# A sixth seven-product pair in the second wide gate of a hybrid encoder layer, with the turning of one block of m moved into that gate

## The chip, the cores and the metric

The kernel runs on one core of one Trainium2 chip. The metric is the time of one execution on the device in microseconds (us). Three executions of the kernel before the change took 1293.12, 1293.61 and 1294.81 us, a median of 1293.61 us. One further execution was recorded by the hardware profiler; all rows of the trace come from that one.

## The reference

One layer on 256 tokens of width 2048, then a final RMSNorm. Only the part around the change is needed:

```python
h = rms_norm(x, g_norm)
proj = h @ w_in                     # uv | q,k,v | gates (2 x 2048 columns)
y_a = gmlp_branch(uv, ...)          # 1024 wide
y_b = neighbourhood_attn(q, k, v, rpb)   # 1024 wide
g_a, g_b = split(sigmoid(gates), 2)
merged = g_a * (y_a @ w_branch[:1024]) + g_b * (y_b @ w_branch[1024:])
x = x + merged @ w_out
x = x + conv_ffn(rms_norm(x))       # up-projection, width-3 convolution, SiLU gate, down-projection
```

Everything is float32. `m` below is `merged`, and a "wide gate" is the right half (1024 of 2048 columns) of `h @ w_in` for `g_a` or `g_b`, before its sigmoid.

## The kernel before, in words

**Products.** A float32 product is made of three TensorE matmuls on halves of the operands (`triple`, L317 to L319: high·high, low·high, high·low). A raw piece of weights `wraw` comes by DMA; ScalarE copies its high part to `whi` (L170), VectorE subtracts to get `wlo` (L171). Activations stand in the same two parts (`h0` to `h7`, a pair of 128-row blocks of k each).

**Steps.** All weights are cut into pieces, numbered through the whole kernel. `begin(i)` issues the load of piece i+5, writes the split of a piece some steps ahead (4 in the wide gates), and then the tasks that were put down for step i by `at(i, ...)`. No scheduler reorders anything: each engine executes its instructions in the order in which the code writes them, step by step. So the number in an `at` decides behind which splits, sums and matmuls a task stands on VectorE, ScalarE, TensorE and in the DMA queue of SyncE (SP).

**A wide gate** (`wide`, `run_wide`) computes 256 x 1024 outputs over k = 2048: 16 pieces of 128 x 1024, taken as 8 pairs in the order of `GATE_ORDER`. C[t][c] are four accumulator banks (row block t, column half c). A plain piece writes four triples, C00, C01, C10, C11, so a plain pair has 24 matmuls. A pair in `GATE_QUADS` (numbered by place) takes seven block products instead of eight, 21 matmuls: in its first piece P0, C00 and C01, in its second P1, P3, P2 and C10, into four more banks P; C11 gets nothing from such a pair. The PSUM pool has 8 banks. When the last such pair is done, `post_sums` (L590 to L594, one ScalarE copy and four VectorE operations) takes P into the gate's tile; `add_sums` (L599, four VectorE operations) adds C at the end of the gate, and a sigmoid (L925) follows on ScalarE.

**Sums for a seven-product pair.** The operands are sums of blocks. Those of the activations are made earlier and kept in DRAM; `kept_sums` reads them back (L1225, tile `s`, 512 KB on SP's queue). Those of the weights are made at the pair by four VectorE additions of 128x512 (`weight_sums`: L363, L364 into `t13`, L360, L361 into `t24`) three pieces ahead, and split two pieces ahead (`weight_sums_split`: ScalarE L374 into h13, h24; VectorE L375 into l13, l24). For the k-pairs 0 and 3 the split weight sums come ready from DRAM instead (`split_read`, L1217, tiles `kh13` and so on), at leads given by `GATE_SPLIT`.

**m.** `ev_branch` multiplies a branch product with its gate, one 512-column block j at a time; for br = 1 it adds the two (`g`, here `g1`). `turn_m(j)` then turns the block: for each half `k2`, four 128x128 transposes on TensorE (L958) into one bank, a ScalarE copy `f` for the later sums (L963), two ScalarE copies of the high parts of `m` (L526) and two VectorE subtractions of the low parts (L531). For block j = 1 this stood at the step ahead of the first piece of the second wide gate: `g_gw[1][1]` is the number of that piece.

Around the change the program goes: first wide gate (gate 0), second wide gate (gate 1), then the remaining branch products, and much later `merged @ w_out`, which reads `m`.

Of the kernel before, what the change touches and what calls it, by code (L numbers as in the profile page):

```python
# [49 lines left out]
GELU_AT = (21, 18)  # L50
X_SUMS = ((1, 5, 6), (2, 12, 13), (6, 18, 19))
GATE_KEPT, GATE_MADE = (1, 2, 6), (0, 3, 4)
GATE_QUADS = ((0, 1, 2, 4, 5, 6), (1, 2, 4, 5, 6))
GATE_ORDER = ((2, 3, 0, 1, 4, 5, 10, 11, 12, 13, 6, 7, 8, 9, 14, 15), (10, 11, 2, 3, 0, 1, 14, 15, 4, 5, 6, 7, 12, 13, 8, 9))
GATE_SPLIT = ({0: (2, 4, 3), 3: (2, 3, 2)}, {0: (2, 4, 3), 3: (2, 1, 1)})
GATE_FIRST = (40, (44, 46, 48, 48), (49, 51))
GATE_JOB = (3, (6, 6, 7, 7), (9, 12))
GATE_SUMS = ((0, 38, 40, "y4", "y5"), (3, 39, 40, "y6", "y7"))
GATE_LATE, Y_LATE = 7, 44
KEEP_AT = (22, 25, 29)  # L60
OUT_PAIRS = (0, 1, 2, 3, 4)
# [17 lines left out]
def trunk_kernel(ctx, tc, x, x_t, vecs, w_in, ln_g, ln_b, w_st, b_s, rpb, w_branch, w_out, w_up, w_down,  # L79
# [26 lines left out]
    def bank():  # L106
        return psum.tile([128, 512], F32, name="bank")
# [10 lines left out]
    def plan_wide(src, row0, order, c0):  # L118
        first = len(pieces)
        for k in order:  # L120
            pieces.append((src, row0 + k * 128, 2, (c0, 512, 1, 0), 512))
        return first
# [66 lines left out]
    def at(i, f):  # L189
        tasks.setdefault(i, []).append(f)  # L190
# [90 lines left out]

    def wide(src, row0, order, c0, acts, quads, room, done, sums=None, stored=None, split=None, late=False, lead=4):
        n0 = plan_wide(src, row0, order, c0)
        boxes = {}
        for q in quads:
            i = n0 + 2 * q
            k = order[2 * q]
            units[i], units[i + 1] = 1, 2  # L290
            b = boxes[q] = {}
            ready = split[0].get(k // 2) if split else None
            if stored:
                b["acts"] = {}
                at(i - (ready[0] if ready else lead), lambda b=b, k=k: stored(k // 2, b["acts"]))
            else:
                b["acts"] = sums[k]
            if ready:
                halved.add(i)
                for n, lead in zip(("13", "24"), ready[-2:]):  # L300
                    at(i - lead, lambda b=b, k=k, n=n: split[1](k // 2, b, n))
                continue
            whole[i] = whole[i + 1] = None
            halves = late and q == quads[0]
            at(i - 3, lambda i=i, b=b, halves=halves: weight_sums(i, b, room, halves))
            if halves:
                at(i - 2, lambda b=b: b.pop("rest")())
            at(i - 2, lambda b=b: weight_sums_split(b, room))
        return ("wide", n0, order, acts, quads, boxes, done)

    def sum_acts_at(i, j, box, pair, room, name, early=False):
# [42 lines left out]
    def weight_sums(i, box, room, halves=False):  # L354
        r0, r1 = whole.pop(i), whole.pop(i + 1)
        t13, t24 = room("t13", F32), room("t24", F32)
        box["w"] = (t13, t24)

        def rest():
            nc.vector.tensor_add(t24[:, 1], t13[:, 0], r1[:, 1])  # L360
            nc.vector.tensor_add(t24[:, 0], r1[:, 0], t24[:, 1])  # L361

        nc.vector.tensor_add(t13[:, 0], r0[:, 0], r0[:, 1])  # L363
        nc.vector.tensor_add(t13[:, 1], r0[:, 1], r1[:, 1])  # L364
        if halves:
            box["rest"] = rest
        else:
            rest()

    def weight_sums_split(box, room):  # L370
        u = []
        for name, t in zip(("13", "24"), box.pop("w")):
            h, l = room("h" + name, F32R), room("l" + name, F32R)
            nc.scalar.activation(h, t, AF.Copy)  # L374
            nc.vector.tensor_sub(l, t, h.bitcast(F32))  # L375
            u.append((h, l))
        split_sums(box, u)

    def split_sums(box, u):
        box["t"] = {1: [x[:, 0] for x in u[0]], 3: [x[:, 1] for x in u[0]],  # L380
                    2: [x[:, 1] for x in u[1]], 4: [x[:, 0] for x in u[1]]}
# [205 lines left out]
    def post_sums(P, x, spare):  # L587
        p1, p5, p6, p7 = P
        (x11, x12), (x21, x22) = x
        nc.scalar.activation(x11, p1, AF.Copy)  # L590
        nc.vector.tensor_sub(spare, x11, p6)
        nc.vector.tensor_add(x12, p5, spare)
        nc.vector.tensor_add(x21, p7, spare)
        nc.vector.tensor_add(x22, p5, x21)  # L594
# [301 lines left out]
    def gate_tile(br):  # L896
        mg["t", br] = mg["p"].tile([128, NT, 1024], F32, name=f"g{br}")
# [10 lines left out]
    def ev_gate_sums(br):  # L908
        def done(P, i):
            def go():  # L910
                gate_tile(br)
                mg["x", br] = [[mg["t", br][:, t, c * 512:(c + 1) * 512] for c in range(2)] for t in range(NT)]
                post_sums(P, mg["x", br], junk)

            at(i + 1, go)
        return done

    def ev_gate_wide(br):
        def done(ps, i):
            g = mg["t", br]  # L920
            add_sums(ps, mg["x", br])

            def sigmoid():
                for t in range(NT):
                    nc.scalar.activation(g[:, t, :], g[:, t, :], AF.Sigmoid, scale=st1["r"][:, t:t + 1])  # L925

            at(i + 1, sigmoid)
            for c in range(2):
                mg[br, 2 + c] = g[:, :, c * 512:(c + 1) * 512]
        return done  # L930

    def ev_branch(br, j):
        def done(ps, i):
            g = mg[br, j]
            for t in range(NT):
                nc.vector.tensor_mul(g[:, t, :], ps[t], g[:, t, :])
            if br == 1:
                for t in range(NT):
                    nc.vector.tensor_add(g[:, t, :], g[:, t, :], mg[0, j][:, t, :])
                at(i + 1 if j == 3 else g_gw[1][1] - 1 if j == 1 else i + 2, lambda: turn_m(j))  # L940
        return done

    def open_m(half):
# [4 lines left out]

    mg["mT"], mg["pairs"] = [], []

    def turn_m(j):
        g = mg[1, j]
        for k2 in range(2):
            p = bank()
            for kk in range(2):
                c = k2 * 2 + kk
                for t in range(NT):
                    nc.tensor.transpose(p[:, kk * T + t * 128:kk * T + (t + 1) * 128],  # L958
                                        g[:, t, c * 128:(c + 1) * 128], ident)
            k = j * 4 + k2 * 2  # L960
            if k // 2 in OUT_PAIRS:
                f = mg["f", k // 2] = mg["fp"].tile([128, 512], F32, name=f"f{k // 2}")
                nc.scalar.activation(f, p, AF.Copy)  # L963
            split_pair(p, mg["mT"][k:k + 2], None)
# [227 lines left out]
    for n, (q, i, j) in enumerate(X_SUMS):  # L1192
        sum_acts_at(i, j, first_sums[2 * q], lambda q=q: q,
                    lambda name, dt, i=i: first_room("s2" if name == "f" and i < 16 else name, dt), f"s{n}", True)
# [27 lines left out]
    def kept_sums(pair, box):  # L1222
# [3 lines left out]
        box["s"] = sums_of(o)  # L1226

    g_gw = [wide(w_in2, 0, GATE_ORDER[br], (GA0, GB0)[br] + 1024, xt, GATE_QUADS[br], sums_room,
                 (ev_gate_sums(br), ev_gate_wide(br)), stored=kept_sums, lead=2,
                 split=(GATE_SPLIT[br], split_read(g_kept, br, lambda pair, name: sums_room("k" + name, F32R), nc.sync)))  # L1230
            for br in range(2)]
    g_m2 = [g_branch(br, j) for j in (2, 3) for br in range(2)]
# [53 lines left out]
    for n, (pair, g) in enumerate((pair, g) for g in range(2) for pair in OUT_SPLIT[g]):  # L1286
        t_kept[pair, g] = split_rows("out", pair, g)
        i = g_at[2 * n][1]
        split_ahead(w_o, t_kept, lambda: at_pool["jobs"], lambda c: f"th{c}", nc.sync, pair, g, g * 1024, i + OUT_JOB[0], [i + a for a in OUT_JOB[1]],
                    [i + a for a in OUT_JOB[2]], 4, last=True)  # L1290
    for n, (pair, br) in enumerate((pair, br) for br in range(2) for pair in GATE_SPLIT[br]):
        g_kept[pair, br] = split_rows("gate", pair, br)
# [66 lines left out]
    def down_order(g):  # L1359
# [194 lines left out]
```

## Time and profile before

| | |
|---|---|
| median of three executions | 1293.61 us (1293.12 to 1294.81) |
| the profiled execution | 1293.75 us, its span 1292.0 us |
| TensorE busy | 1281.9 us of the span |
| VectorE busy | 1140.6 us |
| ScalarE busy | 814.2 us |
| gate 0's last two pieces | 411.93 to 418.26 us |
| gate 1 | 418.26 to 458.38 us |

Times in the trace are in microseconds from the start of the span; a row gives its start, its length, engine, line, operation, output and inputs, and in brackets the idle time before it and what ended it. The executions' times are 1.75 us above the span in the profiled one; that difference lies outside the program's instructions. The profile names lines of the kernel before; in the changed kernel the same statements stand one to five lines lower (L318 to L320 for a triple, L172 for `wlo`, L361 to L365 for the weight sums, L376 for their low parts, L532 for the low parts of `m`, L600 for `add_sums`, L963 for a transpose).

### The profile page before, as it was taken

The numbers are of one execution on the slowest core, as the hardware profiler recorded it, in microseconds if no ns is written. First come the engines' busy times: TensorE is split into PE (matmuls) and PEld (weight loads), VectorE is DVE, ScalarE is ACT, GpSimd is POOL, SyncE is SP. The second block draws the span as 40 slices with busy tenths as digits, with TensorE's granted clock in tenths as the row PEclk, the third lists the DMA queues.
The fourth block names the chain that finished last, engine by engine and source line by source line (L and its number), as shares of the span: only waits on it lengthen the run. The fifth ranks groups of instructions, "written<-read, shape, count | busy, mean of one in ns | idle before, by whom it ended". The sixth has DMA issues, their size and how long they took to land.

```text
span 1292.0 us, 19677 instructions
## 1 busy us (share of the span) xinstructions
PE 1281.9 (99%) x6656; PEld 1093.1 (85%) x6656; DVE 1140.6 (88%) x1707; ACT 814.2 (63%) x1228; POOL 174.6 (14%) x309
## 2 busy tenths in 40 slices
PE   9999999999999999999999999999999999999997
PEld 7888888888888888888888888888888888888885
DVE  7898978888889988997888899898988989989988
ACT  7776577877855645566566656566665656555654
POOL 0003806334000001100001001100000001211210
PEclk9999999999999999999999999999999999999999
DMA  9789879998899977975588788888866859998993
GB/s 368 273 269 280 276 251 301 330 313 299 280 331 355 365 258 239 412 228 163 180 295 274 238 299 292 267 266 286 268 219 221 278 173 360 370 390 320 359 385 142
DMA packets 200182, 370.56 MB, mean 287 GB/s; under 512 B 16017, under 2 KB 124177, under 8 KB 200081
## 3 DMA queue, kind: packets, MB, share of 16 engines
q1 hardware_dynamic: 175616, 287.02, 64.9%
q0 software_dynamic: 23888, 81.23, 17.9%
q8 instruction: 52, 0.85, 0.3%
q10 hardware_dynamic: 576, 1.06, 0.2%
q14 instruction: 50, 0.40, 0.1%
HBM read 321.53 MB, written 45.61 MB: 284 GB/s over the span
## 4 chain that ended last, share of the span: by engine, by line
PE 99%; ACT 0%; DVE 0%; issue 0%
PE bank L222 31%; PE bank L226 16%; PE bank L317 12%; PE bank L319 12%; PE bank L318 12%; PE bank L250 5%; PE bank L252 5%; PE bank L251 5%; PE bank L829 1%; PE bank L879 0%; PE bank L493 0%; PE bank L693 0%; PE bank L869 0%; PE bank L1033 0%; PE bank L958 0%; ACT x L1159 0%
## 5 line engine op out<-in xcount | busy, mean ns | idle before, releaser
L171 DVE TENSOR_TENSOR wlo<-wraw,whi 128x1024 fp32r<-128x1024 f32 (+1 forms) x472 | 538.4, 1153 | 103.6 <-ACT whi L170 69.7
L170 ACT ACTIVATE whi<-wraw 128x1024 fp32r<-128x1024 f32 (+1 forms) x472 | 463.8, 996 | 194.3 <-PE bank L318 88.2
L222 PE MATMUL bank<-h,whi 128*128 128x512 f32 x1760 | 425.5, 392 | 0.0
L222 PEld LDWEIGHTS bank<-h,whi 128*128 128x128 f32 x1760 | 322.0, 188 | 61.8
L226 PEld LDWEIGHTS bank<-h,wlo 128*128 128x128 f32 x1760 | 225.9, 191 | 8.8
L226 PE MATMUL bank<-h,wlo 128*128 128x256 f32 x1760 | 228.6, 283 | 0.0
L1059 ACT ACTIVATE tc<-ta,ck 128x256 f32<-128x256 f32 x86 | 47.1, 595 | 110.4 <-DVE ta L1057 110.4
L317 PE MATMUL bank<-whi,h 128*128 128x512 f32 x192 | 75.3, 392 | 0.0
L319 PE MATMUL bank<-wlo,h 128*128 128x512 f32 x192 | 75.1, 391 | 0.0
L318 PE MATMUL bank<-whi,h 128*128 128x512 f32 x192 | 75.0, 390 | 0.0
L319 PE MATMUL bank<-wlo,a 128*128 128x512 f32 x188 | 73.3, 390 | 0.0
L318 PE MATMUL bank<-whi,a 128*128 128x512 f32 x188 | 73.2, 389 | 0.0
L317 PE MATMUL bank<-whi,a 128*128 128x512 f32 x188 | 73.1, 389 | 0.0
L1062 DVE SCALAR_TENSOR_TENSOR tc<-ta,ck,tc 128x255 f32<-128x255 f32 x86 | 41.4, 482 | 14.4 <-ACT tc L1059 14.4
L794 POOL TENSOR_SCALAR_AFFINE_SELECT bias<-run 64x128 f32<-64x128 f32 x64 | 40.9, 672 | 84.2 <-DVE sc L837 83.6
L1261 POOL DMA_DIRECT2D down_h<-so x16 | 8.7, 543 | 311.2 <-ACT so L1256 198.9
L250 PE MATMUL bank<-whi,y 128*128 128x512 f32 x128 | 50.5, 394 | 0.0
L250 PE MATMUL bank<-whi,h 128*128 128x512 f32 x128 | 50.4, 394 | 0.0
L252 PE MATMUL bank<-wlo,h 128*128 128x512 f32 x128 | 49.9, 390 | 0.0
L252 PE MATMUL bank<-wlo,y 128*128 128x512 f32 x128 | 49.9, 390 | 0.0
L251 PE MATMUL bank<-whi,h 128*128 128x512 f32 x128 | 49.8, 389 | 0.0
L251 PE MATMUL bank<-whi,y 128*128 128x512 f32 x128 | 49.8, 389 | 0.0
(324 smaller groups left out, 2062.8 us busy)
## 6 DMA issues: line engine op xcount, KB each, us to landing
wraw<-in_w_up_dram SPq DMA_DIRECT2D x336, 256.0 KB, 4.2
wraw<-in_w_in_dram SPq DMA_DIRECT2D x107, 512.0 KB, 6.5
wraw<-in_w_down_dram SPq DMA_DIRECT2D x78, 512.0 KB, 7.2
wraw<-in_w_in_dram SPq DMA_DIRECT2D x70, 256.0 KB, 5.9
wraw<-in_w_branch_dram SPq DMA_DIRECT2D x32, 512.0 KB, 6.0
wraw<-in_w_out_dram SPq DMA_DIRECT2D x28, 512.0 KB, 6.0
h<-sums POOLq DMA_DIRECT2D x18, 512.0 KB, 7.6
tw<-in_w_down_dram POOLq DMA_DIRECT2D x8, 1024.0 KB, 8.9
```

The lines of the kernel that those rows point to most:

```text
L170: nc.scalar.activation(h[:, k, :m], w[:, k, :m], AF.Copy)
L171: nc.vector.tensor_sub(l[:, k, :m], w[:, k, :m], h[:, k, :m].bitcast(F32))
L222: nc.tensor.matmul(p, h[:, k - k0, b * 128:(b + 1) * 128], acts(k), start=k == 0, stop=k == nk - 1)
L226: nc.tensor.matmul(p[:, :T], l[:, k - k0, b * 128:(b + 1) * 128], acts(k)[:, 0, :], start=False, stop=False)
L250: nc.tensor.matmul(p, xh, h[:, kk, :m], start=st, stop=False)
L251: nc.tensor.matmul(p, xl, h[:, kk, :m], start=False, stop=False)
L252: nc.tensor.matmul(p, xh, l[:, kk, :m], start=False, stop=sp)
L317: nc.tensor.matmul(p, xh, h, start=st, stop=False)
L318: nc.tensor.matmul(p, xl, h, start=False, stop=False)
L319: nc.tensor.matmul(p, xh, l, start=False, stop=sp)
L1059: nc.scalar.activation(v, u, AF.Identity, scale=ck[:, 1, ch:ch + 1], bias=ck[:, 3, ch:ch + 1])
L1062: nc.vector.scalar_tensor_tensor(v[:, 1:], u[:, :T - 1], ck[:, 0, ch:ch + 1], v[:, 1:], op0=OP.mult, op1=OP.add)
```

## The change

In the second wide gate the pair at place 0 becomes a seven-product pair too, so that both gates have six: one triple less. The order of its pairs changes so that the first is k-pair 4, whose activation sums exist already (they are made for the first gate) and are read from DRAM here once more. Its weight sums are made three pieces ahead as usual, and split one piece ahead instead of two (`behind`). The lead of one read of ready weight sums for k-pair 0 goes from 4 to 3. The turning of block 1 of m leaves the step ahead of the gate: its first half stands at the gate's piece 2, its second half at piece 4.

```diff
-GATE_QUADS = ((0, 1, 2, 4, 5, 6), (1, 2, 4, 5, 6))
-GATE_ORDER = ((2, 3, ...), (10, 11, 2, 3, 0, 1, 14, 15, 4, 5, 6, 7, 12, 13, 8, 9))
-GATE_SPLIT = ({0: (2, 4, 3), 3: (2, 3, 2)}, {0: (2, 4, 3), 3: (2, 1, 1)})
+GATE_QUADS = ((0, 1, 2, 4, 5, 6),) * 2
+GATE_ORDER = ((2, 3, ...), (8, 9, 0, 1, 2, 3, 14, 15, 4, 5, 6, 7, 12, 13, 10, 11))
+GATE_SPLIT = ({0: (2, 4, 3), 3: (2, 3, 2)}, {0: (2, 3, 3), 3: (2, 1, 1)})
+TURN_M = (2, 4)
...
-            at(i - 2, lambda b=b: weight_sums_split(b, room))
+            at(i - (1 if q in behind else 2), lambda b=b: weight_sums_split(b, room))
...
-                at(i + 1 if j == 3 else g_gw[1][1] - 1 if j == 1 else i + 2, lambda: turn_m(j))
+                if j == 1:
+                    for n, k2 in enumerate((0, 1)):
+                        at(g_gw[1][1] + TURN_M[n], lambda k2=k2: turn_m(j, (k2,)))
+                else:
+                    at(i + 1 if j == 3 else i + 2, lambda: turn_m(j))
...
-    def turn_m(j):
-        g = mg[1, j]
-        for k2 in range(2):
+    def turn_m(j, halves=(0, 1)):
+        g = mg[1, j]
+        for k2 in halves:
...
-                 (ev_gate_sums(br), ev_gate_wide(br)), stored=kept_sums, lead=2,
+                 (ev_gate_sums(br), ev_gate_wide(br)), stored=kept_sums, lead=2, behind=((), (0,))[br],
```

**TensorE, before.** Ahead of the last piece of gate 0 (the last triple of the piece before it, and the first of that last piece); `bank_4645` and `bank_4656` take the two halves of m's block 1, a plain name without brackets waits for nothing:

```order
L317 MATMUL bank_4318<-whi_4560,h7_116 128x512
L318 MATMUL bank_4318<-whi_4560,h7_116 128x512
L319 MATMUL bank_4318<-wlo_4561,h7_116 128x512
L958 MATMUL bank_4645<-ident_81,g1_2688 128x128 [waits Activation_49]
L958 MATMUL bank_4645<-ident_81,g1_2688 128x128 x3
L958 MATMUL bank_4656<-ident_81,g1_2688 128x128 [waits DVE_49]
L958 MATMUL bank_4656<-ident_81,g1_2688 128x128 x3
L317 MATMUL bank_4315<-whi_4578,h7_116 128x512
L318 MATMUL bank_4315<-whi_4578,h7_116 128x512
L319 MATMUL bank_4315<-wlo_4579,h7_116 128x512
```

Two halves stand together there, in two different banks.

**TensorE, after.** At piece 4 of gate 1, between its pair 1 (the last triple of that pair, from ready sums `kh24`, `kl24`) and its pair 2; `bank_4790` takes the second half of the block:

```order
L318 MATMUL bank_4689<-kh24_4659,h0_109 128x512
L319 MATMUL bank_4689<-kh24_4659,h0_109 128x512
L320 MATMUL bank_4689<-kl24_4660,h0_109 128x512
L963 MATMUL bank_4790<-ident_81,g1_2688 128x128 [waits DVE_49,Activation_49]
L963 MATMUL bank_4790<-ident_81,g1_2688 128x128 x3
L318 MATMUL bank_4691<-whi_4706,h1_110 128x512
L319 MATMUL bank_4691<-whi_4706,h1_110 128x512
L320 MATMUL bank_4691<-wlo_4707,h1_110 128x512
```

The eight transposes have left the place ahead of gate 0's last piece; four of them now stand at piece 2 (in `bank_4746`, which waits for VectorE) and these four at piece 4, where the first waits for VectorE and ScalarE. The matmuls that follow on TensorE stand behind that wait.

**VectorE, before.** From the last split of gate 0's time to the low parts of the sums of gate 1's first seven-product pair; `t_4639` and `t_4640` are that pair's sums, `m_4178` and `m_4179` the two halves of m's block 1, `g_4615` is gate 0's tile:

```order
L171 TENSOR_TENSOR wlo<-wraw,whi 128x512
L363 TENSOR_TENSOR t_4639<-wraw 128x512
L364 TENSOR_TENSOR t_4639<-wraw 128x512
L360 TENSOR_TENSOR t_4640<-t_4639,wraw 128x512
L361 TENSOR_TENSOR t_4640<-wraw,t_4640 128x512
L531 TENSOR_TENSOR m_4178<-bank,m_4178 128x256 x2
L531 TENSOR_TENSOR m_4179<-bank,m_4179 128x256 x2
L599 TENSOR_TENSOR g_4615<-bank,g_4615 128x512 x4
L171 TENSOR_TENSOR wlo<-wraw,whi 128x1024
L375 TENSOR_TENSOR l_4692<-t_4639,h_4691 128x1024
L375 TENSOR_TENSOR l_4696<-t_4640,h_4695 128x1024
```

**VectorE, after.** From `add_sums` of gate 0 (now `g_4623`) on; `t_4712` and `t_4713` are the weight sums of gate 1's pair 2:

```order
L600 TENSOR_TENSOR g_4623<-bank,g_4623 128x512 x4
L172 TENSOR_TENSOR wlo<-wraw,whi 128x1024
L172 TENSOR_TENSOR wlo<-wraw,whi 128x512
L364 TENSOR_TENSOR t_4712<-wraw 128x512
L365 TENSOR_TENSOR t_4712<-wraw 128x512
L361 TENSOR_TENSOR t_4713<-t_4712,wraw 128x512
L362 TENSOR_TENSOR t_4713<-wraw,t_4713 128x512
L172 TENSOR_TENSOR wlo<-wraw,whi 128x1024
L376 TENSOR_TENSOR l_4739<-t_4712,h_4738 128x1024
L376 TENSOR_TENSOR l_4743<-t_4713,h_4742 128x1024
L532 TENSOR_TENSOR m_4178<-bank,m_4178 128x256 x2
```

The subtractions of m, which stood ahead of `add_sums`, now stand behind it, and behind the sums of pair 2 and their split; the low parts of gate 1's first seven-product pair, which stood behind `add_sums`, now stand ahead of it.

More of the change, by code (lines that the diff above doesn't have):

```diff
@@ L52 @@
 GATE_KEPT, GATE_MADE = (1, 2, 6), (0, 3, 4)
-GATE_QUADS = ((0, 1, 2, 4, 5, 6), (1, 2, 4, 5, 6))
-GATE_ORDER = ((2, 3, 0, 1, 4, 5, 10, 11, 12, 13, 6, 7, 8, 9, 14, 15), (10, 11, 2, 3, 0, 1, 14, 15, 4, 5, 6, 7, 12, 13, 8, 9))
-GATE_SPLIT = ({0: (2, 4, 3), 3: (2, 3, 2)}, {0: (2, 4, 3), 3: (2, 1, 1)})
+GATE_QUADS = ((0, 1, 2, 4, 5, 6),) * 2
+GATE_ORDER = ((2, 3, 0, 1, 4, 5, 10, 11, 12, 13, 6, 7, 8, 9, 14, 15), (8, 9, 0, 1, 2, 3, 14, 15, 4, 5, 6, 7, 12, 13, 10, 11))
+GATE_SPLIT = ({0: (2, 4, 3), 3: (2, 3, 2)}, {0: (2, 3, 3), 3: (2, 1, 1)})
 GATE_FIRST = (40, (44, 46, 48, 48), (49, 51))
@@ L279, in run_group, with wide @@
             done(ps, b)
-    def wide(src, row0, order, c0, acts, quads, room, done, sums=None, stored=None, split=None, late=False, lead=4):
+    def wide(src, row0, order, c0, acts, quads, room, done, sums=None, stored=None, split=None, late=False, lead=4, behind=()):
         n0 = plan_wide(src, row0, order, c0)
```

## The prediction

> **What bounds the kernel now.** I read the page's head first, then the table of TensorE's waits, then the timelines of TensorE, VectorE and ScalarE around the end of gate 0, and the windows over the same stretch. The page's busy time and chain:
>
> ```profile
> PE 1281.9 (99%) x6656; PEld 1093.1 (85%) x6656; DVE 1140.6 (88%) x1707; ACT 814.2 (63%) x1228; POOL 174.6 (14%) x309
> ...
> PE 99%; ACT 0%; DVE 0%; issue 0%
> ```
>
> TensorE is busy 99% of the span and carries the whole chain. The waits of TensorE have one row, at the start of the program:
>
> ```profile
> PE bank L493 <- DVE one L483: 1.5, 1, 1.5
> ```
>
> So TensorE waits for nobody in the stretch of the change, and nothing later can absorb a delay: a matmul fewer is gained in full at the end, a new wait is lost in full. TensorE's rows from the end of gate 0 on (start, length, line, output and inputs):
>
> ```profile
> 411.93 0.39 PE L317 MATMUL bank<-whi,h 128*128 128x512 f32 x1
> ...
> 414.66 1.03 PE L958 MATMUL bank<-ident,g 128*128 128x128 f32 x8
> ...
> 418.26 0.39 PE L317 MATMUL bank<-whi,h 128*128 128x512 f32 x1
> ...
> 458.38 0.39 PE L250 MATMUL bank<-whi,y 128*128 128x512 f32 x1
> ```
>
> 411.93 starts the last two pieces of gate 0 (with the transposes ahead of the second of them), 418.26 gate 1; 458.38 is the first matmul behind gate 1. That gate has three plain pairs of 24 matmuls and five of 21, together 177: 40.12 us / 177 = 0.2267 each. The 0.39 of a row is a latency; starts are what counts. So a plain pair is 24 × 0.2267 = 5.44, a seven-product pair 4.76, a plain piece 2.72. From 414.66 to 418.26 are 3.60 us: a plain piece and eight transposes, hence 0.88 for eight and 0.44 for four.
>
> How near VectorE is to its limit here, by the windows (busy time and instructions of PE, PEld, DVE, ACT, POOL, then clock, DMA share, GB/s):
>
> ```profile
> 407.40:430.40 23.00, 23.00 (x107) 19.15 (x106) 22.28 (x31) 16.93 (x22) 0.00 (x0) 1.00 0.90 329
> 415.00:425.00 10.00, 10.00 (x49) 8.39 (x48) 9.68 (x16) 9.18 (x14) 0.00 (x0) 1.00 1.02 402
> ```
>
> VectorE has 22.28 us of work in 23.0. It is as full as TensorE, but its results are not awaited yet. The change puts more of its work ahead of things that TensorE waits for; that decides the case.
>
> **The triple saved.** 24 matmuls become 21 in pair 0: 3 × 0.2267 = −0.68 us. The transposes are moved, not added.
>
> **VectorE's queue after the change.** Its rows before, which give the price of each kind:
>
> ```profile
> 407.39 4.72 DVE L171 TENSOR_TENSOR wlo<-wraw,whi 128x1024 fp32r<-128x1024 f32 x4
> 412.02 0.68 DVE L591 TENSOR_TENSOR junk<-g,bank 128x512 f32<-128x512 f32 x1
> ...
> 414.06 0.69 DVE L594 TENSOR_TENSOR g<-bank,g 128x512 f32<-128x512 f32 x1
> 415.29 0.69 DVE L171 TENSOR_TENSOR wlo<-wraw,whi 128x512 fp32r<-128x512 f32 x1 [0.53 <-PE bank L958]
> 415.89 0.69 DVE L363 TENSOR_TENSOR t<-wraw 128x512 f32<-128x512 f32 x1
> ...
> 418.43 1.41 DVE L531 TENSOR_TENSOR m<-bank,m 128x256 fp32r<-128x256 f32 x4
> 419.75 2.48 DVE L599 TENSOR_TENSOR g<-bank,g 128x512 f32<-128x512 f32 x4
> 422.14 1.22 DVE L171 TENSOR_TENSOR wlo<-wraw,whi 128x1024 fp32r<-128x1024 f32 x1
> 423.28 2.36 DVE L375 TENSOR_TENSOR l<-t,h 128x1024 fp32r<-128x1024 f32 x2
> ```
>
> By starts: a split of 1024 columns is 1.14 to 1.16 (422.14 to 423.28; 4.63 / 4 at 407.39), one of 512 0.60 (415.29 to 415.89), four weight additions 2.54 (415.89 to 418.43), `post_sums` 2.04 + 0.61 = 2.65, `add_sums` 2.39 (419.75 to 422.14), the low parts of a pair's sums 2.27 (2.36 less the 0.09 by which a row reaches into the next: 2.48 against 2.39 at 419.75), a subtraction of m 1.32 / 4 = 0.33.
>
> In the order after the change I lay these one behind the other from 407.39, where VectorE comes out of the same work as before: two splits of 1024 to 409.71; a split of 512 to 410.31; four additions for pair 0 to 412.85; a split to 413.99; `post_sums` to 416.64; a split of 512 to 417.24; low parts of pair 0 to 419.51; `add_sums` to 421.90; a split of 1024 and one of 512 to 423.64; four additions for pair 2 to 426.18; a split to 427.32; low parts of pair 2 to 429.59; and only then the two subtractions of m's first half, 0.33 and 0.42 (the last with its full latency: row 418.43 lasts 1.41, less 3 × 0.33), to 430.34. About 0.05 us goes for the signal: 430.39.
>
> **TensorE after the change.** Without transposes gate 0 ends at 411.93 + 5.44 = 417.37. Pair 0 has twelve matmuls (P0, C00, C01, P1) to 420.09. Its fifth triple, P3, takes a bank that gate 0's accumulators held until the first `add_sums`; that ends at 419.51 + 0.68 (one such operation's length, as in row 412.02) + 0.05 = 420.24. Wait: **0.15**. Nine more matmuls, 2.04, to 422.28. The first four transposes (0.44, to 422.72) wait for the last `add_sums` at 421.90: no wait. Pair 1, seven products, 4.76, to 427.48. There the second four transposes stand.
>
> Do they wait? All 8 banks are taken from the gate's first piece, 4 P and 4 C. What is left for the turning is the one bank whose accumulator, C11, gets nothing until the plain pair at pieces 6 and 7. Before, the halves had two banks, 4645 and 4656; after, I take both halves to share that one. Then the second half must wait until ScalarE's copies and VectorE's subtractions of the first have read the bank: 430.39. Wait: 430.39 − 427.48 = **2.91**, with everything on TensorE behind it. It is not hidden: the next pair stands in the same queue.
>
> Each of the two waits also bares a weight load. The nearest rows are those of the start, at half the rate:
>
> ```profile
> 1.46 4.02 PE L493 MATMUL bank<-h 128*128 128x512 bf16 x9 [1.46 <-DVE one L483]
> 5.31 0.79 PE L317 MATMUL bank<-whi,h 128*128 128x512 f32 x1
> 5.90 0.63 PE L318 MATMUL bank<-whi,h 128*128 128x512 f32 x1
> 6.34 0.80 PE L319 MATMUL bank<-wlo,h 128*128 128x512 f32 x1
> 6.93 0.52 PE L317 MATMUL bank<-whi,h 128*128 128x512 f32 x1
> ```
>
> There the spacing behind a change of weights is 0.59 (5.31 to 5.90, and 6.34 to 6.93) against 0.44 (5.90 to 6.34), 0.15 more; at the full rate, 0.2267 a matmul, half of it, 0.08 each: **0.16** for two. No row shows a restart at full rate; the ends are zero and 0.15 each, and I take the middle.
>
> **Covers.** ScalarE's rows of this stretch:
>
> ```profile
> 409.78 1.06 ACT L170 ACTIVATE whi<-wraw 128x1024 fp32r<-128x1024 f32 x1 [0.16 <-DMA wraw<-in_w_in_dram]
> ...
> 415.29 0.60 ACT L963 ACTIVATE f<-bank 128x512 f32<-128x512 f32 x1
> 415.78 0.66 ACT L526 ACTIVATE m<-bank 128x256 fp32r<-128x256 f32 x2
> ...
> 419.20 1.99 ACT L374 ACTIVATE h<-t 128x1024 fp32r<-128x1024 f32 x2
> ...
> 423.03 2.20 ACT L925 ACTIVATE g<-g,n_r 128x1024 f32<-128x1024 f32 x2
> ```
>
> Sigmoid can start with `add_sums` at about 420.9 and 421.9 and takes 2.20, to some 423.1; then a copy (1.0) to 424.1. h13 and h24 of pair 2 need VectorE's additions (first sum complete at 424.85, second at 426.18) and end about 426.0 and 427.4; copy f and m's high parts, about 1.1, end at 428.5. VectorE wants them at 429.59: 1.1 us to spare, no cost now; a ScalarE later than that would lengthen the wait one for one. The added read of activation sums (512 KB, 1.3 us of transfer at the 402 GB/s of the window 415 to 425) and its issue on SP's queue hide under the same transfers as long as raw weights land in time; their rival is below. Reading ready sums one piece later, and splitting one piece later (it keeps VectorE's additions of pair 0 ahead of `post_sums`), have their cost in the queue above. Later, VectorE's own delay is used up: before, it idles 2.46 us for ScalarE in row 439.78:
>
> ```profile
> 439.78 1.23 DVE L171 TENSOR_TENSOR wlo<-wraw,whi 128x1024 fp32r<-128x1024 f32 x1 [2.46 <-ACT whi L170]
> ```
>
> Bank C11 is first written by the fourth triple of piece 6, 0.44 + 4.76 + 2.04 = 7.24 us behind the start of the second transposes. Until then the second half is copied (f and the high parts, 1.1) and subtracted behind two splits (2.3 and 0.75): no wait.
>
> **The sum.** −0.68 + 0.15 + 2.91 + 0.16 = +2.54 us. Cross-check: behind the second transposes' start stand 0.44, seven-product pairs and plain pairs 4.76 + 5.44 + 3 × 4.76 + 5.44, together 30.36; 430.39 + 30.36 + 0.16 = 460.91 against 458.38 before: +2.53. The profiled execution, 1293.75, lies 0.14 above the median of 1293.61, so 1293.75 + 2.54 = 1296.29 there and **1296.2** on the median's basis. That is +0.2%, which is also what a measurement of this kernel can just tell from no change: 0.2% is 2.59 us, from 1291.0 to 1296.2.
>
> **The rivals.** *The second half does not wait* (the other side). If the halves get two free banks, as 4645 and 4656 were, or if VectorE reached m's subtraction by 427.5, 2.9 us earlier than my queue says, only −0.68 + 0.15 + 0.08 is left: 1293.2, not slower. For it: rows 414.66 and 418.43 show both halves turned with no wait for a bank. Against: the count of eight banks, and a queue whose every price is a row of the same stretch, 0.7 us of idle in 23. It decides when the subtractions end by 427.48.
>
> *Late raw weights.* The DMA share is at its full 1.02 in 415 to 425, and ScalarE waited 2.87 us for a raw piece, and the kept sums took up to 10.2 us:
>
> ```profile
> 402.12 1.06 ACT L170 ACTIVATE whi<-wraw 128x1024 fp32r<-128x1024 f32 x1 [2.87 <-DMA wraw<-in_w_in_dram]
> ```
>
> ```profile
> DMA to landing us min/median/max: 4.5/7.0/10.2
> ```
>
> The change puts one more read of 512 KB, 1.3 us, into that queue, ahead of raw weights that VectorE wants for pair 2's additions at 423.64. By the landing at 409.78 and 1.3 us for each 512 KB read, about nine and a half of them behind it, pair 2's raw weights land near 422, 1.6 us early. If they come 3.1 us later than that, VectorE slips by 1.5 and the wait grows as much: 1297.7.
>
> *The clock falls in the wait.* At the start matmuls stand 0.43 us apart (nine from 1.46 to 5.31) until 6.93, 5.5 us after the first. If a wait of 2.9 us put TensorE back to that rate, 5.5 / 0.43 = 12.8 matmuls would cost 0.20 more each, +2.6: 1298.8. The waits' table has no such pause, so before cannot show it; the only long pause it shows is that of the start, 1.46, ahead of everything.
>
> The Trainium skill, "TensorE: Matmul & The Clock Gate", section "Part 1: The HAM clock gate (the "warmup" mystery)", states that the clock halves after an idle window of about 3.4 us, free-running, and returns after as long of activity. By it a pause of 2.9 us is too short, though nearly a window, so the sum would stand; the full 3.4 us of slow matmuls would be an estimate of +1.6 instead of +2.6.
>
> **How the numbers follow.** The forecast 0.80; no wait 0.06; late weights 0.08; fallen clock 0.06. The forecast itself lies on the 0.2% line, and I put 0.36 of it below and 0.44 above, since a late ScalarE or DMA lengthens the wait and VectorE had only 0.7 us of idle to lose; a queue of sixteen VectorE terms, each good to 0.03 to 0.05, is good to some 0.7. So same: 0.06 less 0.02 for a measurement that shows more gain than there is, + 0.36 = 0.40, and slower 0.44 + 0.08 + 0.06 = 0.58. Faster by over 0.2% would need −2.6 us where the saving is 0.68: 0.02. The range: below, the forecast less 0.7 and less the 0.5 by which the lowest run lies under the median, 1295.0; left out there is the case without a wait. Above, late weights at 1297.7 and 0.5 of spread, 1298.2; left out is the fallen clock and the tail. Some 0.15 is left out.
>
> **What would show it.** In the profile of the changed kernel the waits of TensorE should have two new groups: one of about 2.9 us at the transposes, ended by VectorE's subtraction of m, one of 0.1 to 0.2 for `add_sums`. VectorE should reach the first subtraction near 429.6 without idling in between, gate 1 should end about 2.5 us later, and stages behind it should be shifted by that alone. No wait at the transposes, an ending of it by ScalarE or a DMA, a clock below 1.00 behind it, or a gain would prove me wrong.

## The result, and the profile after

The changed kernel's ten executions took 1295.35 to 1298.58 us, median 1297.56, against 1293.61 before; the ratio is 1.0026, 95% interval 1.0018 to 1.0035. (The ratio is near that of the means, 1297.18 to 1293.76; the two medians alone would give 1.0031.) Forecast were 1296.2, range 1295.0 to 1298.2. The loss is clear of zero, but its interval reaches down to 0.18%, so it is not told apart from the 0.2% line of the prediction. The profiled execution took 1295.96 us, its span 1294.2, 2.2 more than before. The ten are not one cluster: three lie at 1295.35 to 1295.96 with a mean granted clock (the share of full speed that the throttle granted TensorE) of 0.998, seven at 1297.04 to 1298.58 with 0.996 or 0.997. The profiled one is of the first three; what the seven have in addition is the subject of half of the experiments.

The page's busy time and chain:

```profile
PE 1281.5 (99%) x6653; PEld 1091.7 (84%) x6653; DVE 1144.9 (88%) x1713; ACT 816.3 (63%) x1230; POOL 175.0 (14%) x309
...
PE 96%; DMA 1%; ACT 1%; DVE 1%; issue 0%; ACTq 0%; DVEq 0%; SPq 0%
```

Three matmuls fewer, and about 3% of the chain are no longer TensorE's, where before it had 99%. The waits of TensorE in the changed kernel (us in all, times, longest):

```profile
PE bank L963 <- ACT whi L171: 2.6, 1, 2.6
PE bank L494 <- DVE one L484: 1.5, 1, 1.5
```

One new row, at the transposes (the other is the wait at the program's start). TensorE's timeline:

```profile
411.47 0.39 PE L318 MATMUL bank<-whi,h 128*128 128x512 f32 x1
...
419.40 0.39 PE L320 MATMUL bank<-l,s 128*128 128x512 f32 x1
419.64 0.50 PE L318 MATMUL bank<-h,s 128*128 128x512 f32 x1
419.98 0.39 PE L319 MATMUL bank<-h,s 128*128 128x512 f32 x1
...
421.83 0.60 PE L963 MATMUL bank<-ident,g 128*128 128x128 f32 x4
...
426.84 0.39 PE L320 MATMUL bank<-kl,h 128*128 128x512 f32 x1
429.87 0.63 PE L963 MATMUL bank<-ident,g 128*128 128x128 f32 x4 [2.65 <-ACT whi L171]
430.25 0.48 PE L318 MATMUL bank<-whi,h 128*128 128x512 f32 x1
...
460.31 0.39 PE L251 MATMUL bank<-whi,y 128*128 128x512 f32 x1
```

The stretch from the last two pieces of gate 0 to the end of gate 1 goes from 411.47 to 460.31, 48.84 us, where before it took 46.45 (411.93 to 458.38): +2.39. The first transposes stand without a wait (421.83); the second should start at 426.84 + 0.23 = 427.07 and start at 429.87, 2.80 us later. (The 2.65 in brackets is less because it counts from the modelled end of the row before; in what follows a pause is counted from the time at which TensorE was due.) Behind it the program takes 0.3 us more than before, ahead of it 0.46 less.

VectorE, and one row of ScalarE:

```profile
406.85 2.96 DVE L172 TENSOR_TENSOR wlo<-wraw,whi 128x1024 fp32r<-128x1024 f32 x3
...
418.90 2.48 DVE L600 TENSOR_TENSOR g<-bank,g 128x512 f32<-128x512 f32 x4
...
426.70 2.36 DVE L376 TENSOR_TENSOR l<-t,h 128x1024 fp32r<-128x1024 f32 x2
428.97 0.75 DVE L532 TENSOR_TENSOR m<-bank,m 128x256 fp32r<-128x256 f32 x2
```

```profile
427.74 2.01 ACT L171 ACTIVATE whi<-wraw 128x1024 fp32r<-128x1024 f32 x2
```

VectorE works without a gap from 406.85 to the subtractions of m, which end at 428.97 + 0.75 = 429.72. ScalarE's copies of raw weights end at 429.75, so the row of waits names ScalarE; by 0.03 us the profile cannot tell the two apart. e4, e3 and e11 do.

### The profile page after: what moved, and what is told of

The parts are those of the page before. It is cut to its first block, busy times and chain, and to the rows that moved or that the text cites. A ratio compares the mean times of both kernels' runs of the same rounds, so it can differ in the third digit from the quotient of the medians.

```text
span 1294.2 us, 19695 instructions
## 1 busy us (share of the span) xinstructions
PE 1281.5 (99%) x6653; PEld 1091.7 (84%) x6653; DVE 1144.9 (88%) x1713; ACT 816.3 (63%) x1230; POOL 175.0 (14%) x309
## 4 chain that ended last, share of the span: by engine, by line
PE 96%; DMA 1%; ACT 1%; DVE 1%; issue 0%; ACTq 0%; DVEq 0%; SPq 0%
PE bank L223 31%; PE bank L227 16%; PE bank L320 11%; PE bank L318 11%; PE bank L319 11%; PE bank L251 5%; PE bank L253 5%; PE bank L252 4%; DMA wraw<-in_w_in_dram 1%; PE bank L830 1%; DVE wlo L172 0%; PE bank L880 0%; ACT whi L171 0%; PE bank L494 0%; PE bank L694 0%
## 5 line engine op out<-in xcount | busy, mean ns | idle before, releaser
L318 PE MATMUL bank<-whi,h 128*128 128x512 f32 x186 | 73.2, 394 | 0.0
L320 PE MATMUL bank<-wlo,h 128*128 128x512 f32 x186 | 72.5, 390 | 0.0
L319 PE MATMUL bank<-whi,h 128*128 128x512 f32 x186 | 72.5, 390 | 0.0
L251 PE MATMUL bank<-whi,h 128*128 128x512 f32 x128 | 50.4, 394 | 0.0
L253 PE MATMUL bank<-wlo,h 128*128 128x512 f32 x128 | 49.9, 390 | 0.0
L252 PE MATMUL bank<-whi,h 128*128 128x512 f32 x128 | 49.8, 389 | 0.0
```

The lines of the kernel that those rows point to most:

```text
L251: nc.tensor.matmul(p, xh, h[:, kk, :m], start=st, stop=False)
L252: nc.tensor.matmul(p, xl, h[:, kk, :m], start=False, stop=False)
L253: nc.tensor.matmul(p, xh, l[:, kk, :m], start=False, stop=sp)
L318: nc.tensor.matmul(p, xh, h, start=st, stop=False)
L319: nc.tensor.matmul(p, xl, h, start=False, stop=False)
L320: nc.tensor.matmul(p, xh, l, start=False, stop=sp)
```

## The experiments

Each was run beside the kernel before on the same chip; ratios are against that.

**e1, the change again.**

> The changed kernel once more. Its ten executions fell into two groups: three at 1295.4 to 1296.0 us with a mean clock of 0.998, seven at 1297.0 to 1298.6 with 0.996 or 0.997. Theory (the clock falls in the wait in some executions): the same two groups, about 2 us apart, and the lower clock with the longer time; if the profiled execution is a long one, the wait at the second transposes is still about 2.8 us, but matmuls behind it start some 0.44 us apart for 3.4 to 5.5 us. Rival (raw weights land late in some executions): in a long one the wait itself is 1.5 to 3 us longer, with ScalarE or VectorE waiting for a raw piece, and the spacing behind it stays 0.227.

Nine executions, 1295.80 to 1298.42 us, median 1296.70, ratio 1.0024 (1.0015 to 1.0034). The two groups are there again, though they touch now: 1295.80 to 1296.70 at 0.998, 1296.54 to 1298.42 at 0.996 or 0.997. With the ten above and e8, 20 in all: seven at a clock of 0.998, 1295.35 to 1296.70, median 1295.96; thirteen at 0.996 or 0.997, 1296.54 to 1298.58, median 1297.80. The median of all is 1297.28. The profiled one, 1296.58, belongs to the short ones: its stretch takes 48.87, and its 0.6 over the first trace is a wait near the end of the program (0.64 at 1277.53). So the cause stayed open here.

The mean clock is a coarse sign: 0.997 alone stands also in three of 26 executions of the kernel before, at 1293.45 to 1293.70. Of the thirteen, eight have 0.996.

**e8, a trace of a long execution.** No edit.

> The changed kernel once more, for a trace of a long execution: with about two chances in three its mean clock is 0.996 or 0.997 and its time 1297 to 1298.6 us. Theory (clock): then the wait at the second transposes is 2.6 to 2.8 us as in the short one, and some eight to ten matmuls behind it start 0.43 us apart. Rival: the wait is longer and the spacing 0.227. If it is a short execution it tells nothing new.

It was a long one: 1297.80 us, clock 0.996. Windows of it (busy time of PE, PEld, DVE, ACT, POOL, then clock, DMA share, GB/s), and below them the second window of the short execution shown above:

```profile
426.00:430.00 4.00, 2.08 (x10) 1.38 (x8) 4.00 (x5) 3.73 (x7) 0.00 (x0) 1.00 1.01 352
430.00:436.00 6.00, 5.32 (x20) 4.49 (x21) 5.82 (x10) 3.31 (x7) 0.00 (x0) 0.72 0.77 260
```

```profile
430.00:436.00 6.00, 6.00 (x29) 5.01 (x29) 5.97 (x10) 3.89 (x7) 0.00 (x0) 1.00 0.76 252
```

TensorE's rows behind the pause in the long execution:

```profile
427.69 0.39 PE L320 MATMUL bank<-kl,h 128*128 128x512 f32 x1
430.68 1.08 PE L963 MATMUL bank<-ident,g 128*128 128x128 f32 x4 [2.61 <-ACT whi L171]
431.42 0.78 PE L318 MATMUL bank<-whi,h 128*128 128x512 f32 x1
431.99 0.63 PE L319 MATMUL bank<-whi,h 128*128 128x512 f32 x1
432.42 0.63 PE L320 MATMUL bank<-wlo,h 128*128 128x512 f32 x1
432.85 0.63 PE L318 MATMUL bank<-whi,h 128*128 128x512 f32 x1
433.27 0.53 PE L319 MATMUL bank<-whi,h 128*128 128x512 f32 x1
433.64 0.40 PE L320 MATMUL bank<-wlo,h 128*128 128x512 f32 x1
...
434.57 0.39 PE L318 MATMUL bank<-h,s 128*128 128x512 f32 x1
```

The wait is 430.68 − 427.92 = 2.76, no longer than in the short one. Behind it the granted clock is 0.72 over the window, matmuls start 0.43 apart until 433.27, and then 0.23 again. From the transposes to the tenth matmul behind them are 3.89 us, against 2.56 in the short trace (429.87 to 432.43): the fall of the clock costs 1.33. The whole stretch took 50.69, 1.85 more than in the short one; the other 0.5 is in pair 0, where VectorE came 0.5 later and TensorE's wait for `add_sums` was 0.35 instead of next to nothing. VectorE had lost that time before the stretch began, waiting for a raw piece; first the short execution, then the long one:

```profile
401.50 0.69 DVE L365 TENSOR_TENSOR t<-wraw 128x512 f32<-128x512 f32 x1 [0.77 <-DMA wraw<-in_w_in_dram]
```

```profile
402.32 0.69 DVE L365 TENSOR_TENSOR t<-wraw 128x512 f32<-128x512 f32 x1 [1.27 <-DMA wraw<-in_w_in_dram]
```

So in this execution the rival of late data has a small share, the clock the larger. It is the only trace of a long one; for the other twelve the fall is inferred from the mean clock and the time.

**e4, a longer pause.** The second half one piece earlier, in the middle of pair 1.

```diff
-TURN_M = (2, 4)
+TURN_M = (2, 3)
```

> The second half of the block is turned one piece earlier (piece 3, in the middle of pair 1). TensorE arrives there 2.72 us sooner and VectorE's subtractions come at the same time, so the wait grows to about 5.6 us and +2.54 to +5.3. Theory (clock): with a pause that long the clock falls in every execution, 1.7 to 2.6 us more: 1300.5 to 1301.5 us in all of them, clock 0.996 or 0.997, and the trace shows matmuls some 0.44 us apart behind the pause. Rival (no clock effect; the long executions of the change come from late weights): 1298.9, the spacing behind the pause 0.227.

All five executions lie at 1300.97 to 1301.69 us, median 1301.29, clock 0.995 to 0.997, ratio 1.0059 (1.0045 to 1.0073). The wait, rows behind it, and the window:

```profile
PE bank L963 <- DVE m L532: 5.2, 1, 5.2
```

```profile
429.93 1.09 PE L963 MATMUL bank<-ident,g 128*128 128x128 f32 x4 [5.17 <-DVE m L532]
430.67 0.78 PE L318 MATMUL bank<-kh,s 128*128 128x512 f32 x1
431.25 0.63 PE L319 MATMUL bank<-kh,s 128*128 128x512 f32 x1
431.67 0.63 PE L320 MATMUL bank<-kl,s 128*128 128x512 f32 x1
...
434.23 0.63 PE L320 MATMUL bank<-kl,s 128*128 128x512 f32 x1
434.66 0.47 PE L318 MATMUL bank<-kh,h 128*128 128x512 f32 x1
```

```profile
430.00:435.00 5.00, 5.00 (x15) 4.09 (x16) 2.90 (x4) 2.09 (x4) 0.00 (x0) 0.52 0.51 159
```

Here the row of waits names VectorE's subtraction of m: it ends at 429.04 + 0.75 = 429.79, 0.14 ahead of the transposes, while ScalarE's copy had ended at 428.87:

```profile
429.04 0.75 DVE L532 TENSOR_TENSOR m<-bank,m 128x256 fp32r<-128x256 f32 x2
```

TensorE is 5.3 us late (429.93 for 424.36 + 0.23 = 424.59), and the clock is low for 4.7 us behind it (429.93 to 434.66). From the transposes to the tenth matmul are 4.73, 2.17 more than the 2.56 of the short execution. The other four executions have no trace; their times lie within 0.8 us of this one, at a clock of 0.995 to 0.997.

**e5 and e2, the pause filled.** Matmuls with a zero operand, added to the running bank of P0, between pair 1 and the second transposes, 28 of them in e2 and 11 in e5 (the lines of e2):

```diff
+            if q == 1 and n0 == g_gw[1][1]:
+                for _ in range(AWAKE):
+                    nc.tensor.matmul(P[0][:, :128], nil.to_broadcast([128, 128]), ident, start=False, stop=False)
```

> The changed kernel with 28 matmuls of a zero operand (128 columns, added to a bank that is being accumulated, so nothing is added) between gate 1's pair 1 and the second transposes: by rows of the same kind, 0.09 us each, they fill 2.5 of the 2.8 us in which TensorE waits, and the wait that is left is about 0.3. Nothing else is moved. Theory (clock): every execution at 1295.3 to 1296.1 us, clock 0.998, median 1295.7, some 1.9 under the changed kernel's 1297.56. Rival (late weights): the same spread as without them, median about 1297.5.

e2 missed: 1302.23 us (1301.95 to 1302.70), ratio 1.0066 (1.0054 to 1.0079). The filler was too long:

```profile
429.03 6.41 PE L434 MATMUL bank<-ident,nil 128*128 128x128 f32 x56
```

28 of them are 56 instructions and 6.25 us (to the transposes at 435.28), 3.45 more than the wait. The stretch is 3.9 us longer than in the first trace of the change (412.96 to 465.68); of the other 2.9, 1.5 stand ahead of it and 1.4 behind. There is no pause at the transposes, and all five executions have a clock of 0.998. The zero was a new tile of 4 bytes a partition, which moved the buffers allocated behind it; whether that is the cause of the 2.9 was not tried.

> The filler of e2 mended: 11 matmuls of a zero operand instead of 28 (e2 showed each to be two instructions of 0.111 us), and the zero taken from a tile that exists already, so that no other buffer moves. 22 x 0.111 = 2.45 us of the wait of 2.80 are filled, the pause that is left is about 0.35. Theory (the clock falls in the pause in some executions): no execution has a mean clock of 0.996 or 0.997, all lie between 1295.3 and 1296.8 us, median 1295.9, under the 1297.1 that is the middle of the change's 19 executions so far. Rival (something else makes the long executions): the spread stays, 1295.4 to 1298.6, median near 1297.

Here the zero is a column of an existing tile, `pad`, set by one more VectorE instruction at the start of gate 0:

```profile
427.45 2.62 PE L436 MATMUL bank<-ident,pad 128*128 128x128 f32 x22
430.25 0.63 PE L969 MATMUL bank<-ident,g 128*128 128x128 f32 x4 [0.19 <-ACT whi L172]
```

The pause is 0.35 us by the fillers' 0.111 each (0.19 by the row). Ten executions, all with a clock of 0.998 or 0.999, none over 1297.48: the low clock is gone, though the transposes start as late as before and the stretch takes 48.88, against 48.84. In time the gain is not shown. The median, 1296.73, is 0.8 above the expected 1295.9, five of the ten lie above the 1296.8 that was to be the highest, and the ratio, 1.0024 (1.0015 to 1.0033), is that of e1. Of the 0.5 by which the profiled one (1296.46) exceeds the first trace, 0.34 stands ahead of the last two pieces of gate 0; what the filled version loses elsewhere is open. So e5 shows that the low clock goes with the pause; what it costs is read from e8's rows.

**e3, VectorE's queue.** Pair 2's weight sums are split one piece later, which puts m's subtractions ahead of its low parts.

```diff
-                 ... behind=((), (0,))[br],
+                 ... behind=((), (0, 2))[br],
```

> The weight sums of gate 1's pair 2 are split one piece later too, so that on VectorE the first half's subtractions of m stand ahead of that pair's low parts (2.27 us). Theory (VectorE's queue sets the wait): the wait at the second transposes falls from 2.8 to about 0.6 us, the low parts of pair 2 come just in time, and the sum is -0.68 + 0.15 + 0.6 + 0.16 = +0.2: 1293.8 us, all executions within 0.7 of it, clock 0.998. Rival (the wait is for ScalarE's copies of raw weights, as the trace's row names): these stand where they stood, the wait stays above 2 us, and the median above 1295.

1293.74 us, 1293.07 to 1294.66 in eleven executions, ratio 0.9999 (0.9990 to 1.0008), clock 0.998 or 0.999. The wait and VectorE's row:

```profile
PE bank L963 <- DVE m L532: 0.4, 1, 0.4
```

```profile
426.64 0.75 DVE L532 TENSOR_TENSOR m<-bank,m 128x256 fp32r<-128x256 f32 x2
```

The subtractions came 2.33 us sooner (426.64 for 428.97), and TensorE is 0.53 us late instead of 2.80. But `weight_sums_split` has operations on ScalarE too, and with them ScalarE's copies of raw weights moved as well: the one ahead of the transposes ends at 425.92 here. So e3 alone does not separate the two engines; e11 moves VectorE only.

**e11, a pause between.** e3 with two idle subtractions ahead of m's.

```diff
+                        if n == 0:
+                            at(g_gw[1][1] + TURN_M[n], lambda: [nc.vector.tensor_sub(junk, junk, junk) for _ in range(2)])
```

> e3 with two idle subtractions (0.61 us each) on VectorE ahead of those of m's first half: the wait at the second transposes should be 0.45 + 1.2 = 1.65 us, between those of e3 (never a low clock in 11 executions) and of the change (a low clock in 13 of 20). Time without a fall of the clock 1293.7 + 1.2 = 1294.9 us. If the clock falls after a pause of any length beyond about 1.5 us, some executions are at 0.996 or 0.997 and 1.3 us longer; if it needs more than 2 us, none is.

```profile
428.98 0.63 PE L965 MATMUL bank<-ident,g 128*128 128x128 f32 x4 [1.70 <-DVE m L532]
```

TensorE is 1.85 us late (428.98 for 427.13), 1.32 more than in e3, for two subtractions that take 1.33 on VectorE ahead of those of m:

```profile
428.09 0.75 DVE L532 TENSOR_TENSOR m<-bank,m 128x256 fp32r<-128x256 f32 x2
```

Five traces side by side, with the end of VectorE's subtractions, the end of ScalarE's last copy of raw weights ahead of the transposes, and the start of the transposes:

| | VectorE | ScalarE | transposes |
|---|---|---|---|
| the change | 429.72 | 429.75 | 429.87 |
| e8 | 430.54 | 430.56 | 430.68 |
| e4 | 429.79 | 428.87 | 429.93 |
| e3 | 427.39 | 425.92 | 427.53 |
| e11 | 428.84 | 428.59 | 428.98 |

The transposes start 0.14 to 0.15 us behind VectorE in all five, and 0.12 to 1.61 behind ScalarE. VectorE's queue sets the wait; ScalarE's name in the row of the change is a coincidence.

The eleven executions lie at 1294.79 to 1296.08, median 1295.10, ratio 1.0009 (1.0000 to 1.0018). Three have a clock of 0.997, at 1295.04 to 1295.40, in the middle of the others, and the profiled one of these has matmuls 0.23 us apart behind the pause, so no fall of the kind of e8 is seen.

**e6 and e10, the first half written sooner.** The same place on TensorE, but ahead of the next step's split on VectorE.

```diff
-                    for n, k2 in enumerate((0, 1)):
-                        at(g_gw[1][1] + TURN_M[n], lambda k2=k2: turn_m(j, (k2,)))
+                    at(g_gw[1][1] + 4, lambda: turn_m(j, (1,)))
...
+            if q == 0 and n0 == g_gw[1][1]:
+                turn_m(1, (0,))
```

> The first half is turned at the same place on TensorE (between pair 0 and pair 1), but written before the next step begins, so that on VectorE its subtractions stand ahead of a split (1.14 us) and of pair 2's low parts (2.27). Theory (VectorE's queue alone sets the wait): 3.4 us earlier is more than the wait of 2.8, TensorE does not wait at the second transposes, and what is left is -0.68 + 0.15 + 0.08: 1293.3 us on the basis of 1293.7 before, all executions at clock 0.998. Rival (the bank or ScalarE's copies of raw weights set it): a wait of over 1 us stays, 1295 or more.

No wait at the transposes (VectorE's subtractions stand at 425.60 now):

```profile
427.11 0.60 PE L964 MATMUL bank<-ident,g 128*128 128x128 f32 x4
```

But only four of eleven executions came near 1293.3; seven lie at 1294.49 to 1295.56, median 1294.81, ratio 1.0006 (0.9997 to 1.0014), with no low clock.

> e6 once more, for a trace of one of its longer executions: four of its eleven were at 1293.1 to 1293.8 us, seven at 1294.5 to 1295.6, all with a clock of 0.997 to 0.999. Theory (raw weights or kept sums that land late): in a longer one TensorE has a wait of 1 to 2 us somewhere behind the transposes or in pair 0, ended by a split whose raw piece or sum landed late. Rival (the clock): no such wait, and a stretch of matmuls 0.43 us apart.

On another chip the median is 1293.80 (1293.10 to 1295.14), ratio 0.9999 (0.9991 to 1.0008), and the profiled execution was a longer one, 1295.09:

```profile
450.08 0.50 PE L318 MATMUL bank<-whi,s 128*128 128x512 f32 x1 [1.13 <-DMA s<-xsums]
```

Kept activation sums for a later pair of the gate landed 1.13 us too late. In this execution, with TensorE ahead, a read on SP's queue was the next bound. The profiled execution of e6 was a short one, so the longer ones on its chip have no trace.

**e9, e3 and e6 together.**

> e3 and e6 together: the first half is written ahead of the next step, and the weight sums of pair 2 are split one piece later. Theory: the same time as e6 by the queues, -0.68 + 0.15 + 0.08, 1293.3 us, with 2.3 us more of slack for m on VectorE and less for pair 2's low parts. If e6's executions of 1294.5 to 1295.6 come from m or its bank being late, they are absent here; if they come from data that land late, they stay.

1293.54 us, 1292.56 to 1294.41, ratio 0.9995 (0.9986 to 1.0004): the lowest ratio of all versions, but not told apart from e3, e10 or the kernel before. One execution of eleven lies above 1294.2, against four of e10 on the same chip, though nothing in the reads was changed; why is open. The list of TensorE's waits has no row but that of the start, and the stretch takes 46.46, as before (46.45), with three matmuls fewer. The 0.68 us saved went into small things, by TensorE's rows: a wait and a restart of 0.3 in pair 0 (predicted 0.15 + 0.08), 0.24 for the late sums at a later pair, and slightly wider spacing behind each.

**e7, the quads alone.** The sixth pair, with the turning left ahead of gate 0's last piece.

> The sixth seven-product pair with its order, its reads and its later split, and the turning left where it was before, ahead of gate 0's last piece. Theory (the loss is all in the turning's new place): no wait at the transposes; VectorE does m's four subtractions (1.3 us) ahead of the new pair's low parts, so TensorE waits about 0.7 us in pair 0 instead of 0.15: -0.68 + 0.7 + 0.08 = +0.1, 1293.8 us, clock 0.998. Rival (the sixth pair's own work is what makes VectorE late and costs 2 us): 1295.5 or more.

1294.33 us (1293.45 to 1295.57), ratio 1.0005 (0.9996 to 1.0014), 0.5 above the expectation, and at the transposes no wait. The wait in pair 0 shows:

```profile
420.64 0.47 PE L318 MATMUL bank<-whi,s 128*128 128x512 f32 x1 [0.85 <-ACT whi L171]
```

It stands at the product C01, before the place forecast, and ends with ScalarE's row, not VectorE's as the expectation had it: ScalarE's copies of m stand ahead of that split there. The stretch takes 47.60. So without the moved turning the change costs 0.05%, not told apart from nothing. With e3, which moves m's subtractions forward and costs nothing either, most of the 0.26% comes from where these subtractions stand on VectorE after the move, and from the low clock behind the wait that they make.

## Why the prediction was right, and where it was not

- **Bound.** Right: nothing behind the gate took up the delay; +2.39 in the stretch is +2.2 in the span.
- **The two halves share a bank, and wait for VectorE's subtraction.** Right. The wait was to be 2.91 us and is 2.80; the subtraction was to end 430.34 − 407.39 = 22.95 us behind the same split, and ended 429.72 − 406.85 = 22.87 behind it. Each price of the queue was a row of the same stretch, and it held. e11 and the five traces show that the wait is VectorE's; that the halves wait on each other because they share the one bank rests on the count of eight, which no run varied. The 0.05 us for the signal was low: it is 0.14 to 0.15 in all five traces, and the 0.08 by which VectorE was early made up for most of it. The rival that the second half does not wait is ruled out for the change, and e6's shorter executions, 1293.13 to 1293.77, show what it would have given.
- **Pair 0.** Forecast 0.15 for `add_sums` and 0.08 for the restart; from 419.40 to 419.98 are 0.58 for two spacings of 0.45 in all, 0.13 for both, and 0.16 with the slightly wider spacings up to 421.83. In e8 it was 0.35 and more: it varies from one execution to the next.
- **Restart.** Forecast 0.08 each. From the start of the second transposes to the end of the gate are 30.44 us (429.87 to 460.31), against 30.36 + 0.08 forecast: the same. The four transposes took 0.38 of it instead of 0.44, the rest 0.14 more than the matmuls' own time. The prediction took the price from rows at half rate, as no row showed a restart at the full one; the trace before has one that comes near, behind its transposes, with 0.31 to the next start, 0.08 more than usual:

```profile
415.45 0.48 PE L317 MATMUL bank<-whi,h 128*128 128x512 f32 x1
415.76 0.40 PE L318 MATMUL bank<-whi,h 128*128 128x512 f32 x1
```

- **The sum.** +2.54 forecast, +2.39 in the stage. The sum counts one restart too many: that of pair 0 only makes TensorE come later to a wait whose end VectorE sets, so 0.08 of it is taken up there, and the terms give +2.46. In the whole execution it is 1295.96 − 1293.75 = +2.2, since all ahead of the stage was 0.46 us shorter (411.47 for 411.93) and all behind it 0.3 longer.
- **The clock.** This step failed in its chance: the rival "the clock falls in the wait" had 0.06, and by the mean clock it came in 13 of 20 executions, so that the median holds it. I had set a pause of 2.9 us just under what a fall would need, on no row at all; the only pause of before was the one at the start. Its price was forecast as +2.6 at most, or +1.6; it is 1.33 in e8's trace and 1.84 between the medians of the two groups, of which some is late data. The forecast value 1296.2 describes the short executions. The median lies 1.36 above it, and the range held it only because it reached up for late weights, having left the fallen clock out: that part is luck.
- **Late weights.** As a cause of the long executions nearly wrong: e8's wait at the transposes is no longer, and a raw piece that came late cost it 0.5 in pair 0. As a hazard right in another place: kept sums land late once TensorE is early (e10).

The Trainium skill, "TensorE: Matmul & The Clock Gate", section "Part 1: The HAM clock gate (the "warmup" mystery)", asks for an idle window of about 3.4 us before the clock halves. Here a pause of 2.8 us was enough, in e8's rows and by the mean clock in 13 of 20 executions, so the measurement decides; that it was not enough in seven fits the free-running window of which the section speaks, but no run here shows the window itself.

## What to carry to other kernels

When an operation moves to a later place, list every instruction that stands ahead of it on each engine that its result passes through; the sum of those rows gave this wait to 0.1 us, and one line that put two subtractions ahead of two others (with ScalarE's part of the same split) left 0.5 us of it. Where a wait is ended by another engine, do not add delays that come ahead of it on the waiting one: the wait takes them up. A new pause on a TensorE that has none can cost more than its length: at 2.8 us the clock fell behind it in part of the executions here, at 1.9 us in none: give such a case a chance from the pause's length, not from the absence of such a pause in the trace before. And three matmuls saved were worth nothing that could be measured in e9, where two short waits with their restarts took most of their place.

## What the runs showed of the hardware

- The clock by the time that TensorE was late, one length per version: 0.35 us (e5) and 0.53 us (e3), mean clock 0.998 or more in 10 and 11 executions; 1.85 us (e11), no lengthening in 11; 2.8 us (the change), 0.997 or less in 13 of 20; 5.3 us (e4), in 5 of 5. Rows show the slow stretch in e8, some 3 us long, and in e4, 4.7 us, with matmuls of 512 columns 0.43 us apart in place of 0.227.
- Each filler, a float32 matmul with 128 columns and one broadcast operand, counts as two instructions of 0.111 us each (e2: 28 are 56, in 6.25 us). The transposes, 128 columns too, count as one of 0.09 to 0.10 us (four in 0.36 to 0.38).
- The first matmul behind a short wait or a group of transposes takes 0.31 to 0.34 us to the next start, and some of the following 0.23 to 0.24, where 0.227 is usual (the change: 419.64 to 421.83 is 2.19 for nine, 430.25 to 432.43 is 2.18, in place of 2.04): a restart cost 0.14 to 0.15 us, behind next to no wait as behind one of 2.8.
